# Two FFN output products computed as seven block products each, in a diffusion layer on one core

## The chip, the cores and the metric

The kernel runs on one core of a Trainium2 chip. Its engines are TensorE (PE; its weight loads are shown apart as PEld), VectorE (DVE), ScalarE (ACT), GpSimd (POOL) and SyncE (SP), which here issues all DMAs. The metric is the device time of one execution in microseconds (us); lower is better. For the kernel before, the median of three runs is 2811.78 us (2809.13 to 2812.79).

## The reference, cut to what matters

The program is one layer over 1024 latent tokens with a prefix of 256 context tokens, model width 1024, hidden width of the FFN 2816. All data is fp32. In short:

```python
def swiglu(h, w_in, w_out):
    a, b = jnp.split(h @ w_in, 2, axis=-1)
    return (jax.nn.silu(a) * b) @ w_out

x  = x  + 0.5 * ml[2] * swiglu(modulate(rms_norm(x,  norm1_g), ml[0], ml[1]), ffn1_w_in, ffn1_w_out)
cx = cx + 0.5 * mc[2] * swiglu(modulate(rms_norm(cx, norm1_g), mc[0], mc[1]), ffn1_w_in, ffn1_w_out)
...                     # short convolution and grouped-query attention, merged, added to x
x  = x  + 0.5 * ml[8] * swiglu(modulate(rms_norm(x,  norm3_g), ml[6], ml[7]), ffn2_w_in, ffn2_w_out)
return rms_norm(x, final_g)
```

`ml` and `mc` are nine rows of modulation, `silu(c) @ w_mod + b_mod`, for latent and context tokens. The change concerns the product with `w_out` (2816 x 1024) in the two FFNs over the latent tokens.

## The kernel before, in words

**Layout.** Activations lie transposed: 128 channels on the partitions, tokens along the free dimension. The 1024 tokens are two chunks of 512, C0 and C1. `x` has 8 blocks of 128 channels (KD = 8), the hidden activation `hid` has 22 (NH = 22).

**Precision.** Every fp32 operand is split into a high part (an ACT cast to the fp32r type) and a low part (a DVE subtraction) by `split` (line 186). A block product is three matmuls: high x high, high x low, low x high (`mm3`, line 218). One matmul multiplies a 128x128 block of weights with a 128x512 block of tokens into one PSUM bank.

**Buffers.** 38 tiles of 128x1024 with the tag `A` (`atile`) hold what lives long. `raw` has three buffers of that size for weights as loaded, `wh` and `wl` four each for split operands (W_BUFS, line 39), `t` eleven of 128x512. Of the eight PSUM banks, `ps_s` rotates over five, `ps_t` over two, `ps_o` has one (lines 121 to 128). A framework (Tile) places the semaphores and orders each engine's instructions, by the order of the program and by when an instruction can start in its own model; the queue of SP, which issues the DMAs, is in order as well.

**First halves of the FFNs.** `h @ w_in` is already a product of 2x2 blocks in seven block products (`class Winograd`, line 463): over the pair of column blocks of `w_in` that give `a` and `b`, the halves of the model width, and the two token chunks. `keep` holds the split sums of activations (r1 to r7, four `A` tiles each), `lefts` loads and prepares weights, with sums on GpSimd, `start` computes products 1 and 2 of the first few blocks while `norm1` still makes the other operands, and `second` and `third` do products 6, 7, 4, 5, 3 and add them up on DVE. Each product takes 12 matmuls.

**Second half of FFN 1** (lines 1026 to 1066). The hidden activation was spilled to DRAM (`spill`, line 963, into `hd`). For each token chunk, `hs` loads the 22 blocks of `hid` and splits them, once per chunk. Then, for three, three and two of the eight output blocks `ds`, one `ps_s` bank per block sums up 22 x 3 matmuls, with the weights loaded by `load_w` in columns of 128. An eviction on DVE (`scalar_tensor_tensor`: bank times gate plus `x`) writes `x`, which is stored to `xd`. Beside this the loop drives other work: `run(steps, 4)` in C0 finishes the modulation rows (`later_mod`, line 261: eight loads of 128x512, eight multiply-adds on DVE, two matmuls, per half row), and in C1 `run(norms2, 1)` makes the first operands of the mixing stage from C0 (`norm0`, line 499). After each C1 block, `mix.square(d)` (line 514) adds to the sum of squares that `norm1` (line 525) needs.

**FFN 2** (`ffn`, line 742, called in line 1522). Here the two halves are interleaved: for each of 11 pairs of hidden blocks, the seven products of `w_in` are done for two blocks, `hidden` splits the result and keeps it in SBUF, `out_pieces` (line 451) loads and splits the two row blocks of `w_out`, and for both chunks and all eight output blocks six matmuls go into a bank, which DVE adds to `x` times the gate at once. So `x` is evicted to once per pair, 176 times and more. For the last pair, C1 goes in two parts of 256 tokens (`last_chunks`), and `after2` starts the final norm of the parts that are done (`final`, line 1488): squares and scaled copies on ACT, additions on DVE and GpSimd, column sums on TensorE, a Newton iteration of small DVE operations, transposes on TensorE, scaling, and the store of the output.

The profile gives line 88 for nearly all instructions, because one helper issues them. Groups are told apart by tiles.

Of the kernel before, what the change touches and what calls it, by code (L numbers as in the profile page):

```python
# [9 lines left out]
F32 = mybir.dt.float32  # L10
# [3 lines left out]
ALU = mybir.AluOpType  # L14
# [35 lines left out]
def tile_dit_layer(  # L50
# [79 lines left out]
    def matmul(out, w, x, start, stop, pinned=False):  # L130
        inst = pe.matmul(out, w, x, start=start, stop=stop)
        if pinned:
            tc.keep_in_program_order(inst)
# [329 lines left out]
    class Winograd:  # L463
# [6 lines left out]
        def __init__(self, xs, gain, mod, m, pairs, plain=False, ahead=3, side_from=None):  # L470
# [9 lines left out]
            self.n_ahead, self.side, self.started, self.n_left = ahead, None, [], 0  # L480
            self.source, self.ready = self.lefts(pairs, side_from), []
# [32 lines left out]
        def square(self, d):  # L514

            if d == 0:
                self.acc = [ttile("sq_acc")]
            sq = self.acc[0] if d == 0 else ttile("sq")
            act.activation(out=sq, in_=self.xs(d, C1), func=AF.Square)
            if d == KD - 1:  # L520
                self.acc.append(sq)
            elif d:
                dve.tensor_add(out=self.acc[0], in0=self.acc[0], in1=sq)

# [217 lines left out]
        def ffn(self, w_o, gate, last_chunks, after):  # L742
            def hidden(a, b, j, ch):

                if j % 2 == 0:
                    t = atile("hid", (P, 2, 512), F32R)
                    g = t[:, 0], t[:, 1]
                else:
                    g = ttile("gh", dt=F32R), ttile("gl", dt=F32R)
                act.activation(out=a, in_=a, func=AF.Silu)  # L750
                dve.tensor_mul(out=a, in0=a, in1=b)
                split(a, *g)
                hid[j, ch] = g

            for pr in range(NH // 2):
                hid = {}
                js = (2 * pr, 2 * pr + 1)
                if pr == 0:
                    self.start(self.norm1())
                for j in js:  # L760
                    u, c = self.next_first()
                    v, b = self.second(u)
                    hidden(c, b, j, C0)
                    hidden(*self.third(u, v), j, C1)
                ws = out_pieces(w_o, js)
                if pr < NH // 2 - 1:
                    self.prefetch(3)
                for ch in (C0, C1) if pr < NH // 2 - 1 else last_chunks:
                    s, o, n = ch
                    full = (C0, C1)[o // 512]  # L770
                    a = o - full[1]
                    for dt in range(KD):
                        po = ps_s(n)
                        c = (dt % 4) * P
                        terms = []
                        for j in (2 * pr, 2 * pr + 1):
                            wt = ws[j, dt // 4]
                            gh, gl = hid[j, full]
                            terms.append((wt[:, 0, c : c + P], wt[:, 1, c : c + P], gh[:, a : a + n], gl[:, a : a + n]))
                        mm3(po, terms)  # L780
                        dve.scalar_tensor_tensor(
                            out=xs(dt, ch), in0=po, scalar=gate[:, dt : dt + 1], in1=xs(dt, ch),
                            op0=ALU.mult, op1=ALU.add,
                        )
                        if pr == NH // 2 - 1:
                            after(ch, dt)
# [242 lines left out]
    for ch in (C0, C1):  # L1029
        o = ch[1]  # L1030
        hs = []
        for j in range(NH):
# [542 lines left out]
```

## Time and profile before

| | before |
|---|---|
| median of 3 runs | 2811.78 us (2809.13 to 2812.79) |
| the profiled execution's own time | 2810.07 us |
| its span, from the first to the last instruction | 2808.1 us |
| mean granted TensorE clock | 0.984 |
| DMA | 302.96 MB, mean 108 GB/s |

How to read it: the page shows one execution. A row of a group gives the engine, the operation, output and inputs by the program's names, the shape, the count, then the busy time, the mean length of one, and the idle time of that engine just before, with what ended it. In a row of a window, each engine's busy time stands with its count of instructions, then the granted TensorE clock (1.00 is full), the share of time in which the DMA engines were busy, and GB/s. Matmuls overlap in the pipeline, so their price is taken from the number that run in a stretch in which TensorE is busy throughout. A row for a DMA ends with the median time from issue to landing. The lines themselves stand in the prediction.

### The profile page before, as it was taken

What the parts mean: (1) busy time and instruction counts of PE and PEld (TensorE: products, weight loads), DVE (VectorE), ACT (ScalarE), POOL (GpSimd) and SP (SyncE); (2) the same over time, 40 slices, a digit from 0 to 9 for tenths busy, and PEclk for the clock granted to TensorE, in tenths of its full rate; (3) what the DMA queues carried; (4) which work ended last, traced back from release to release, by engine and by line L of the source; (5) the groups of instructions that cost most, each with busy time, mean ns of one, the idle gap of its engine ahead of it and who ended that gap; (6) DMA issues with size and microseconds to landing.
All of it is one profiled execution on the core that took longest, in us unless ns stands there. A gap on an engine that the chain in (4) does not pass through costs nothing.

```text
span 2808.1 us, 37023 instructions
## 1 busy us (share of the span) xinstructions
PE 2719.5 (97%) x13741; PEld 2283.1 (81%) x13741; DVE 1953.1 (70%) x3194; ACT 1105.0 (39%) x2177; POOL 586.7 (21%) x458
## 2 busy tenths in 40 slices
PE   7898999999999989999999999999998999999998
PEld 4687988888888868888999888877886788888887
DVE  5887688877864397676568676675458766666667
ACT  4524333333433243323344665674235212332225
POOL 2541122121001063323123111000014221212111
PEclk8899999999999989999999999999999999999999
DMA  8364434445974333322312321002432311111111
GB/s 304 101 200 149 144 109 126 130 143 160 311 240 127 102 119 108 102 74 91 108 44 76 102 79 42 31 31 75 162 91 90 110 41 53 60 56 58 46 53 68
DMA packets 355229, 302.96 MB, mean 108 GB/s; under 512 B 25558, under 2 KB 284776, under 8 KB 355048
## 3 DMA queue, kind: packets, MB, share of 16 engines
q1 hardware_dynamic: 355048, 300.59, 33.3%
q8 instruction: 108, 1.77, 0.3%
q14 instruction: 73, 0.60, 0.1%
HBM read 251.73 MB, written 48.76 MB: 107 GB/s over the span
## 4 chain that ended last, share of the span: by engine, by line
PE 81%; DVE 11%; DMA 4%; issue 2%; ACT 2%; POOL 1%; SPq 1%; DVEq 0%; ACTq 0%; POOLq 0%
PE ps L88 71%; PE po L88 6%; PE pt L88 4%; DVE wl L88 2%; DVE r L88 1%; DMA rawm<-in_w_mod_dram 1%; DVE nt L88 1%; DVE macc L88 1%; DMA raw<-in_ffn_w_out_dram 1%; DVE wo L88 1%; DVE uc L88 1%; DVE u L88 1%; DMA hid<-hd 1%; DVE h L88 1%; SPq L88 1%
## 5 line engine op out<-in xcount | busy, mean ns | idle before, releaser
L88 PE MATMUL ps<-r,wl 128*128 128x512 f32 x5280 | 1240.9, 394 | 36.6 <-ACT wl L88 13.2
L88 PEld LDWEIGHTS ps<-r,wl 128*128 128x128 f32 x5280 | 994.8, 190 | 255.7 <-ACT wl L88 17.2
L88 ACT CAST wl<-s 128x512 fp32r<-128x512 f32 x256 | 158.6, 620 | 335.4 <-PE ps L88 273.3
L88 ACT CAST wl<-raw 128x512 fp32r<-128x512 f32 x230 | 142.4, 620 | 243.5 <-PE ps L88 162.4
L88 DVE TENSOR_TENSOR wl<-raw,wl 128x512 fp32r<-128x512 f32 x228 | 168.2, 738 | 98.3 <-ACT wl L88 97.2
L88 POOL TENSOR_TENSOR s<-raw,s 128x512 f32<-128x512 f32 x64 | 98.6, 1541 | 621.4 <-DVE wl L88 617.3
L88 DVE TENSOR_TENSOR wl<-s,wl 128x512 fp32r<-128x512 f32 x256 | 214.7, 840 | 11.6 <-ACT wl L88 9.8
L88 PE MATMUL ps<-hid,wh 128*128 128x512 f32 x704 | 217.3, 390 | 0.6 <-ACT wh L88 0.6
L88 DVE SCALAR_TENSOR_TENSOR x<-ps,gate_l,x 128x512 f32<-128x512 f32 (+1 forms) x200 | 141.0, 726 | 81.2 <-PE ps L88 81.0
L88 POOL TENSOR_TENSOR s<-raw 128x512 f32<-128x512 f32 x64 | 90.8, 1419 | 401.8 <-DMA raw<-in_ffn_w_in_dram 163.9
L88 ACT CAST wh<-raw 128x1024 fp32r<-128x1024 f32 (+2 forms) x92 | 89.4, 976 | 196.5 <-PE ps L88 162.6
L88 PEld LDWEIGHTS ps<-hid,wh 128*128 128x128 f32 x704 | 131.8, 188 | 29.2 <-ACT wh L88 1.3
L88 DVE SCALAR_TENSOR_TENSOR macc<-rawm,silu_c,macc 128x512 f32<-128x512 f32 x168 | 141.6, 861 | 11.9 <-DMA rawm<-in_w_mod_dram 10.5
L88 PE MATMUL ps<-hid,wo 128*128 128x512 f32 (+1 forms) x552 | 147.8, 381 | 1.8 <-DVE x L88 1.8
L88 DVE TENSOR_TENSOR u<-u,ps 128x512 f32<-128x512 f32 x168 | 114.5, 681 | 49.7 <-PE ps L88 48.1
L88 POOL TENSOR_TENSOR sq_acc<-sq_acc,sq 128x512 f32<-128x512 f32 (+1 forms) x33 | 41.5, 1258 | 505.3 <-ACT sq L88 504.4
L88 DVE TENSOR_TENSOR wl<-raw,wh 128x1024 fp32r<-128x1024 f32 (+1 forms) x84 | 99.9, 1190 | 64.1 <-ACT wh L88 62.8
L88 PE MATMUL ps<-wh,r 128*128 128x256 f32 x768 | 141.6, 285 | 0.0
L88 DVE TENSOR_TENSOR pts<-pt,pts 128x512 fp32r<-128x512 f32 x160 | 108.7, 687 | 42.6 <-ACT pts L88 41.4
L88 PE MATMUL ps<-hid,wl 128*128 128x512 f32 x352 | 136.5, 389 | 0.0
L88 PE MATMUL ps<-gh,wo 128*128 128x512 f32 (+1 forms) x368 | 135.0, 380 | 0.0
L88 DVE TENSOR_REDUCE m<-ps 128x1 f32<-128x512 f32 (+1 forms) x192 | 111.1, 596 | 27.1 <-PE ps L88 26.1
(260 smaller groups left out, 4922.6 us busy)
## 6 DMA issues: line engine op xcount, KB each, us to landing
raw<-in_ffn_w_in_dram SPq DMA_DIRECT2D x114, 512.0 KB, 3.9
raw<-in_ffn_w_out_dram SPq DMA_DIRECT2D x76, 512.0 KB, 4.6
rawm<-in_w_mod_dram SPq DMA_DIRECT2D x128, 256.0 KB, 4.2
raw<-in_w_in_dram SPq DMA_DIRECT2D x57, 512.0 KB, 4.2
hid<-hd SPq DMA_DIRECT2D x44, 256.0 KB, 6.1
rawm<-in_w_mod_dram SPq DMA_DIRECT2D x16, 512.0 KB, 7.9
xd<-x SPq DMA_DIRECT2D x32, 256.0 KB, 8.6
x<-xd SPq DMA_DIRECT2D x32, 256.0 KB, 5.7
```

The source lines that it names most:

```text
L88: inst = getattr(self.engine, name)(*args, **kw)
```

## The change

Both products `w_out^T x hid` become products of 2x2 blocks: rows of `w_out` (hidden blocks 0 to 10 and 11 to 21), columns of `w_out` (output blocks 0 to 3 and 4 to 7), and token chunks. Seven block products with sums of operands take the place of eight. A new function, `row_products`, does them in the order 1, 2, 5, 6, 7, 3, 4. Products 1, 6, 7 and 4 add up one on another in four `ps_s` banks (`chain`), read after each; products 2, 5 and 3 use the other four banks. `Rows` holds the hidden activation in SBUF, unsplit, in tiles of two row blocks. For each group of two row blocks (five, and one of a single block) `operands` loads parts of `w_out` (`part_of_w`), splits both operands into `wl` and `wh`, and makes the sums for later products on DVE, in place.

In FFN 1 the modulation steps that ran in the old loop move into the loop of the mixing stage, and `norm0` of that stage moves into product 4. In FFN 2 the hidden activation is now spilled to DRAM for all blocks first and loaded again; the seven products follow. The last product there is done in two halves of 256 tokens, with split operands kept in `A` tiles, and the final norm runs beside it. In `final`, the scaled copies go from ACT to DVE, the sums of squares from GpSimd to DVE and to more matmuls, and one of two banks changes.

```diff
+    def row_products(w, rows, add, after=lambda i, k: None, halves=False):
+        R, groups = P * rows.n, rows.groups
+        sums = {}
+        def part_of_w(k, m, lower, left):
+            t = wpool.tile([P, 2, 512], F32, tag="raw", name=uniq("raw"), bufs=3)[:, :m]
+            o, c = k * P + R * lower, 512 * (not left)
+            load(t, w[o : o + m * P, c : c + 512].rearrange("(a p) n -> p a n", p=P))
+            return t
...
+        def operands(i, k, m, tags=("wl", "wh")):
+            b11, b12, b21, b22 = (rows.t[k, v, c] for v in range(2) for c in (1, 0))
+            if i == 1:
+                left = part_of_w(k, m, 0, True)
+            elif i == 2:
+                left = part_of_w(k, m, 1, True)
+            elif i == 7:
+                left, a21 = part_of_w(k, m, 0, True), part_of_w(k, m, 0, False)
+                dve.tensor_sub(out=left, in0=left, in1=a21)
+            elif i == 4:
+                left = part_of_w(k, m, 1, False)
+            else:
+                left = sums[k]
+            right = {1: b11, 2: b21, 5: b11, 6: b11, 7: b12, 4: b11, 3: b22}[i]
+            l, r = parts(left, m, tags[0]), parts(right, m, tags[1])
+            if i == 1:
+                dve.tensor_sub(out=b11, in0=b12, in1=b11)
+            elif i == 2:
+                sums[k] = atile("ws", (P, 2, 512))[:, :m]
+                a21, a22 = part_of_w(k, m, 0, False), part_of_w(k, m, 1, False)
+                dve.tensor_add(out=sums[k], in0=a21, in1=a22)
+            elif i == 5:
+                a11 = part_of_w(k, m, 0, True)
+                dve.tensor_sub(out=sums[k], in0=sums[k], in1=a11)
+                dve.tensor_sub(out=b11, in0=b22, in1=b11)
+            elif i == 6:
+                a12 = part_of_w(k, m, 1, True)
+                dve.tensor_sub(out=sums[k], in0=a12, in1=sums[k])
+                dve.tensor_sub(out=b12, in0=b22, in1=b12)
+            elif i == 3:
+                dve.tensor_sub(out=b11, in0=b21, in1=b11)
+            return l, r
+        def steps_of(i, ps, k, m, l, r, a=0, n=512):
+            for e in range(m):
+                for d in range(4):
+                    wh, wl = (t[:, e, d * P : (d + 1) * P] for t in l)
+                    xh, xl = (t[:, e, a : a + n] for t in r)
+                    on = i in (6, 7, 4)
+                    matmul(ps[d], wh, xh, start=not on and k + e == 0, stop=False, on=on)
+                    matmul(ps[d], wh, xl, start=False, stop=False, on=on)
+                    matmul(ps[d], wl, xh, start=False, stop=k + e == rows.n - 1, on=on)
+        chain = [ps_s() for _ in range(4)]
+        for i in (1, 2, 5, 6, 7, 3):
+            ps = chain if i in (1, 6, 7) else [ps_s(), ps_t(), ps_t(), ps_o()]
+            for k, m in groups:
+                steps_of(i, ps, k, m, *operands(i, k, m))
+                after(i, k)
+            for d in range(4):
+                if i in (1, 2):
+                    add(d, C1, ps[d])
+                elif i == 5:
+                    add(d, C0, ps[d])
+                    add(d + 4, C0, ps[d])
+                elif i in (6, 3):
+                    add(d, C0, ps[d])
+                elif i == 7:
+                    add(d + 4, C0, ps[d])
+            after(i, rows.n)
...                      # then product 4, for FFN 2 in two halves of 256 tokens
@@ FFN 1
+    hs = Rows(NH // 2, "hid")
+    hs.fetch(hd)
...
+        if i == 4 and k in (0, 2, 4, 6):
+            run(norms2, 1)
+    row_products(ffn1_w_out[0], hs, add1, after1)
@@ the loop of the mixing stage
         run(normc2, 2)
+        run(steps, 9)
@@ FFN 2
-    fast.ffn(ffn2_w_out[0], gate3["l"], last_chunks, after2)
+    fast.start(fast.norm1())
+    for j in range(NH):
+        u, c = fast.next_first()
+        v, b = fast.second(u)
+        spill(c, b, j, C0)
+        spill(*fast.third(u, v), j, C1)
+    hs = Rows(NH // 2, "hid")
+    hs.fetch(hd)
...
+    def after3(i, k):
+        if i == 9 and k < NH // 2:
+            run(finals[0], 3)
+        if (i, k) == (8, NH // 2):
+            run(finals[0], 2)
+        if i == 9 and k >= 4 and k < NH // 2:
+            run(finals[1], 4)
+        if (i, k) == (9, NH // 2 - 1):
+            run(finals[2], 4)
+    row_products(ffn2_w_out[0], hs, add3, after3, halves=True)
```

More of the change, by code (lines that the diff above doesn't have):

```diff
@@ L740, in third @@
             return u, v
[L742 to L786, printed above, removed]
```

153 lines of the change are left out of this document (99 added, 54 removed).

## The prediction

> **What bounds the kernel now.** I read the page first: busy time by engine, the strip of granted clock, the chain that ended last.
>
> ```profile
> span 2808.1 us, 37023 instructions
> PE 2719.5 (97%) x13741; PEld 2283.1 (81%) x13741; DVE 1953.1 (70%) x3194; ACT 1105.0 (39%) x2177; POOL 586.7 (21%) x458
> PEclk8899999999999989999999999999999999999999
> GB/s 304 101 200 149 144 109 126 130 143 160 311 240 127 102 119 108 102 74 91 108 44 76 102 79 42 31 31 75 162 91 90 110 41 53 60 56 58 46 53 68
> PE 81%; DVE 11%; DMA 4%; issue 2%; ACT 2%; POOL 1%; SPq 1%; DVEq 0%; ACTq 0%; POOLq 0%
> ```
>
> TensorE is busy 97% of the span and carries 81% of the chain, nearly always at full clock. That is an average, so next come the windows, cut at the stages that the change touches: the first FFN's output product (722.8 to 966.8), the start and the body of the mixing stage, the start, body and end of the second FFN, and a stretch of 256-wide matmuls.
>
> ```profile
> core 0: us, PE busy (x) PEld busy (x) DVE busy (x) ACT busy (x) POOL busy (x), PEclk, DMA share, GB/s
> 722.80:966.80 244.00, 243.44 (x1079) 200.15 (x1078) 131.43 (x175) 83.22 (x112) 12.64 (x7) 1.00 0.62 198
> 966.80:1040.00 73.20, 60.95 (x242) 46.32 (x241) 59.81 (x83) 32.81 (x61) 36.31 (x26) 0.88 0.33 108
> 1040.00:1370.00 330.00, 330.00 (x1459) 273.15 (x1458) 238.68 (x357) 108.46 (x180) 107.64 (x75) 1.00 0.31 98
> 2107.20:2200.00 92.80, 79.48 (x331) 62.25 (x330) 78.27 (x104) 43.67 (x75) 37.48 (x25) 0.93 0.32 104
> 2200.00:2770.00 570.00, 569.54 (x2511) 470.70 (x2510) 375.93 (x539) 153.90 (x262) 103.08 (x75) 1.00 0.18 54
> 2770.00:2808.10 38.10, 30.05 (x215) 27.25 (x213) 29.00 (x78) 27.51 (x57) 8.54 (x9) 0.96 0.27 111
> 1450.00:1500.00 50.00, 50.00 (x422) 50.00 (x421) 40.49 (x109) 22.97 (x88) 17.74 (x37) 1.00 0.14 44
> ```
>
> Both output products run where TensorE never rests (243.44 of 244.00; 569.54 of 570.00). A matmul left out there is time gained, as long as the engines that feed it keep up. DVE is busy 131 of the first 244 us, 376 of the 570. For the price of a 512-wide matmul I want a stretch that holds little else:
>
> ```profile
> 2600.00:2650.00 50.00, 50.00 (x222) 41.42 (x221) 31.30 (x46) 15.95 (x27) 7.15 (x6) 1.00 0.18 53
> ```
>
> 50.00 / 222 = **0.225 us** per 512-wide matmul, and 50.00 / 422 = **0.118 us** per 256-wide one (the row 1450 to 1500). The 389 ns that the groups below show for one is its length in the pipeline, not its price.
>
> **The change part by part.** First the matmuls that exist now, by shape:
>
> ```profile
> L88 PE MATMUL ps<-hid,wh x704: 387/389/504, 722.8 to 966.2; 128*128 128x512 f32 x176
> L88 PE MATMUL ps<-hid,wl x352: 387/389/398, 724.3 to 966.4; 128*128 128x512 f32 x176
> L88 PE MATMUL ps<-hid,wo 128*128 128x512 f32 x504 | 139.3, 390 | 1.8 <-DVE x L88 1.8
> L88 PE MATMUL ps<-gh,wo 128*128 128x512 f32 x336 | 126.7, 389 | 0.0
> L88 PE MATMUL ps<-gl,wo 128*128 128x512 f32 x168 | 64.9, 389 | 0.0
> L88 PE MATMUL ps<-hid,wo 128*128 128x256 f32 x48 | 8.5, 286 | 0.0
> ```
>
> FFN 1: 704 + 352 = 1056 of width 512. FFN 2: 504 + 336 + 168 = 1008 of width 512 and 96 of width 256 (48 in the row, 48 with the other two operands). After: each of seven products has 11 row blocks x 4 column blocks x 3 terms = 132 matmuls, 924 in all. In FFN 2 the last product runs in two 256-wide halves: 792 + 264.
>
> - FFN 1: (1056 - 924) x 0.225 = **-29.7 us**.
> - FFN 2: (1008 - 792) x 0.225 = 48.6, less (264 - 96) x 0.118 = 19.8: **-28.8 us**.
>
> That is -58.5 us if TensorE stays as busy as now. What feeds it decides the rest:
>
> ```profile
> L88 DVE TENSOR_TENSOR wl<-raw,wh 128x1024 fp32r<-128x1024 f32 x68 | 84.5, 1245 | 30.3 <-ACT wh L88 29.1
> L88 ACT CAST wh<-raw 128x1024 fp32r<-128x1024 f32 x68 | 71.2, 1051 | 148.2 <-PE ps L88 120.7 <-DMA raw<-in_ffn_w_out_dram 15.0 <-DMA raw<-in_w_in_dram 8.0
> L88 DVE SCALAR_TENSOR_TENSOR x<-ps,gate_l,x 128x512 f32<-128x512 f32 x184 | 133.5, 748 | 80.1 <-PE ps L88 80.1
> raw<-in_ffn_w_out_dram SPq DMA_DIRECT2D x76, 512.0 KB, 4.6
> rawm<-in_w_mod_dram SPq DMA_DIRECT2D x16, 512.0 KB, 7.9
> hid<-hd SPq DMA_DIRECT2D x44, 256.0 KB, 6.1
> ```
>
> A product is 5.5 groups of two row blocks; a group is 24 matmuls, 5.4 us. Only two groups fit the four `wl` and four `wh` buffers, so the feed may lag by one group at most.
>
> *DVE.* Each group takes two subtractions for the low parts, and sums that prepare later products: 3, 3, 4, 4, 3, 3 and 2 operations of 1024 elements in products 1, 2, 5, 6, 7, 3, 4. That is 22 x 5.5 x 1.245 = 151 us, and 32 evictions of 0.748 us make 24: 175 of 208 us. It fits as a whole. In 5 and 6 it doesn't: 4 x 5.5 x 1.245 = 27.4, plus 4 evictions of product 2 (30.4) and 8 of product 5 (33.4), against 29.7 of matmuls. The excess is 4.4 us; part of it is hidden by the lead. I take 2 (bounds 0 and 4.4). ACT casts 14 x 5.5 x 1.051 = 81 us: not a bound.
>
> *Loads.* Product 2 loads three pieces of `w` per group (its own operand and the two of the sum) through three `raw` buffers. Each buffer's round is landing 4.6 + cast 1.05 + subtraction 1.25 = 6.9 us, against 5.4: 1.5 x 5.5 = 8 us late, less up to one group of lead. I take 5 (bounds 0 and, with the 7.9 us row, 21). Product 7 loads two: one buffer is held for 4.6 + 1.25 + 1.05 + 1.25 = 8.2 us, the other for 4.6 + 1.25 = 5.9; over three buffers that is 14.1 / 3 = 4.7 us per group, just under 5.4. I take 1. On SP's queue these loads stand behind the `xd` stores in FFN 1, which wait for evictions; that wait is in the bounds.
>
> For the landing, the Trainium skill, "DMA: Bandwidth & Descriptors", Anatomy of one DMA — SWDGE (gpsimd) path, gives 2.0 us plus bytes over 436 GB/s, an estimate of 3.2 us here; by that product 2 would hide its loads and the sum would be 10 us lower for the two stages. It is fitted on another path, and the 4.6 us row is what I go by.
>
> *Handovers.* Product 5 takes over the banks of 2, and 7 goes on in those of 6. The last group has 12 matmuls in four banks, so bank 0 is done 9 x 0.225 = 2.0 us before the end, and evictions of 0.748 us follow the matmuls at nearly their pace. The new wait stands on TensorE with all later matmuls behind it; it costs little only if DVE is free at that moment. I take 3 per stage, the stage's entry with it (bounds 0 and 11: four evictions, then a load of 6.1 and its split). At the entry of FFN 2 the `hid` tiles need slots of the 38 `A` tiles: 8 hold `x`, 28 hold `r`, so the loads start as the last block's `r` come free, ahead of need in the order of product 1.
>
> *Clock.* 1 us per stage, since waits this short left the clock at 1.00 in the rows above.
>
> New waits: 2 + 5 + 1 + 3 + 1 = **12 us per stage, +24**.
>
> *Around the stages.* (a) FFN 1's stage is now 244.0 for 1056 x 0.225 = 237.6 us; of the other 6.4, 23 more matmuls take about half (six of full width and smaller ones, an estimate), and about 3 us are waits, which my 12 replace: **-3**. (b) The last 63 steps of the modulations move into the mixing body: three half rows, 24 operations on DVE by this row, and 24 loads of 256 KB on SP:
>
> ```profile
> L88 DVE SCALAR_TENSOR_TENSOR macc<-rawm,silu_c,macc 128x512 f32<-128x512 f32 x168 | 141.6, 861 | 11.9 <-DMA rawm<-in_w_mod_dram 10.5
> ```
>
> 24 x 0.861 = 21 us beside 330 us in which DVE is busy 239. TensorE hides it; if that cover is gone it costs 21. **+2**. (c) `norm0` of the mixing stage is squeezed from the second column chunk's 122 us (half of 244) into product 4's 30, and four squares come after the last matmul instead of one: its start, which already loses time (60.95 of 73.20, clock 0.88), begins later: **+3** (bounds 0 and 10). (d) In FFN 2 the first half now runs unbroken; the hidden splits and 184 evictions leave DVE, two loads and stores of `hd` are added and hide under matmuls: 0. (e) The end: four adds in place of one after the last matmul, but fewer additions of squares: 0 (bounds -2 and +4).
>
> Sum against the profiled execution: 2808.1 - 58.5 + 24 - 3 + 2 + 3 = 2775.6 us of span. That execution took 2810.07 us, 2.0 above its span, and the median shown is 1.7 above that: 2775.6 + 3.7 = **2779 us**.
>
> **The rivals.**
>
> *All hidden.* The loads run ahead and DVE's lag is covered; only entries, handovers and the clock cost, 4 per stage instead of 12, and (b) is free: 2775.6 - 16 - 2 + 3.7 = **2761**. For it: the mixing body runs at 330.00 of 330.00 with the same kind of feed. Against it: product 2 asks for 1.5 MB in 5.4 us, 290 GB/s, and the densest slices of the strip (around this stage, and at the kernel's start) moved 311 and 304.
>
> *The `raw` ring binds (slower).* If three loads in flight land in 7.9 us, product 2's round is 10.2 against 5.4 and costs 4.8 x 5.5 - 5.4 = 21; product 7's is (11.4 + 9.1) / 3 = 6.9 and costs 8. That is 23 more per stage than I took: **2825**. Against 2811.78 it decides from a landing of about 6.8 us on, between the two rows. For it: 7.9 stands in this trace for loads of this size in a burst. Against it: those are the loads at the kernel's start, where many more than three are queued at once.
>
> *The clock falls.* Here waits on the feed coincide with a lower granted clock:
>
> ```profile
> 200.00:250.00 50.00, 40.30 (x182) 32.81 (x181) 42.03 (x79) 19.45 (x39) 17.59 (x16) 0.86 0.41 127
> 450.00:500.00 50.00, 49.37 (x280) 42.67 (x279) 38.12 (x61) 17.11 (x31) 8.38 (x5) 1.00 0.32 95
> 1000.00:1050.00 50.00, 41.43 (x145) 30.21 (x146) 45.29 (x65) 20.66 (x39) 29.10 (x22) 0.83 0.36 117
> ```
>
> At 80% busy the clock was 0.86 and 0.83, at 99% it was 1.00. If products 2 and 7 run at 0.85, their 59 us of matmuls take 10.5 more per stage: 2779 + 21 = **2800**. The Trainium skill, "TensorE: Matmul & The Clock Gate", A second HAM failure mode: psum-queue depth-cycling, says that cycling through PSUM banks with short rests between groups made the clock swing; it speaks for this case. Against it: the present stage also changes banks, and stood at 1.00.
>
> *It doesn't do what it says*: fewer matmuls are certain from the code; I give it nothing.
>
> **How the numbers follow.** Forecast (2765 to 2795) 0.51, all hidden 0.21, clock falls 0.12, ring binds 0.16. About 0.2% (6 us) is what a measurement of this kernel can tell from no change. Ring bound ends within 0.2% in a fifth of its cases: 0.03; the clock case is nearly always faster. So faster 0.82, same 0.04, slower 0.14. The range takes in the hidden case and most of the ring's: 2754 to 2822.
>
> **What would show it.** Matmuls: 924 per stage, TensorE's idle time there mostly before product 2, with `raw` loads ending it, then before 5 and 7 with evictions ending it. DVE near 85% busy in the stage and close to full in products 5 and 6. The stage's length near 222 us instead of 244. A landing of `raw` above 6.8 us, or a granted clock below 0.95 in the stages, would make the prediction wrong upward; a stage below 213 us, downward.

## The result, and the profile after

| | before | after |
|---|---|---|
| median of 20 runs each | 2813.21 us (2809.13 to 2821.24) | 2817.73 us (2814.79 to 2824.51) |
| span of the profiled execution | 2808.1 us | 2814.9 us |
| mean granted TensorE clock | 0.984 | 0.979 |

The ratio of after to before is 1.002, 95% interval 1.0014 to 1.0026. The kernel became about 0.2% slower. The time lies in the range on record, but the forecast had said faster. Against the forecast span of 2775.6 us, 39.3 us have to be found.

The page of the kernel after: span, TensorE's busy time, its granted clock in 40 slices, and the chain that ended last.

```profile
span 2814.9 us, 36971 instructions
PE 2689.3 (96%) x13625; PEld 2253.9 (80%) x13625; DVE 2014.9 (72%) x3166; ACT 1129.9 (40%) x2141; POOL 582.5 (21%) x449
PEclk8899999999999989999999999999999999999999
PE 77%; DVE 11%; DMA 6%; issue 3%; ACT 2%; POOL 1%; SPq 1%; DVEq 0%; ACTq 0%; POOLq 0%
```

TensorE is busy 30 us less (2719.5 before), and yet the span is 7 us longer: its idle time grew by 37 us, from 88.6 to 125.6. Where, is read from four marks on TensorE: the first and last matmul of FFN 1's output product, the first matmul after the mixing loop (operand `h2ch`), and the last before FFN 2 (operand `mh`). Rows by tile, with the first and last start in us; the kernel after:

```profile
L88 PE MATMUL ps<-wh,wl x627: 387/389/629, 724.0 to 959.4; 128*128 128x512 f32 x157
L88 PE MATMUL pt<-wh,wl x198: 387/389/628, 757.6 to 926.3; 128*128 128x512 f32 x198
L88 PE MATMUL po<-wh,wl x99: 388/389/398, 758.5 to 926.7; 128*128 128x512 f32 x99
L88 PE MATMUL ps<-wh,h2ch x32: 278/283/363, 1387.0 to 1421.4; 128*128 128x256 f32 x32
L88 PE MATMUL ps<-mh,wl x128: 387/389/477, 2033.5 to 2121.3; 128*128 128x512 f32 x128
```

The same two marks in the kernel before:

```profile
L88 PE MATMUL ps<-wh,h2ch x32: 277/283/363, 1372.2 to 1406.4; 128*128 128x256 f32 x32
L88 PE MATMUL ps<-mh,wl x128: 387/389/477, 2019.2 to 2106.9; 128*128 128x512 f32 x128
```

627 + 198 + 99 = 924 matmuls: the count is as forecast. The stretches between the marks (before: 722.8, 966.4, 1372.2, 2106.9, 2808.1):

| stretch | before | forecast | after | missed by |
|---|---|---|---|---|
| up to the output product | 722.8 | 722.8 | 724.0 | +1.2 |
| FFN 1's output product | 243.6 | 222.9 (−29.7 + 12 − 3) | 235.4 | **+12.5** |
| start and loop of the mixing stage | 405.8 | 410.8 (+2 + 3) | 427.6 | **+16.8** |
| from there to FFN 2 | 734.7 | 734.7 | 734.3 | −0.4 |
| FFN 2 and the end | 701.2 | 684.4 (−28.8 + 12) | 693.6 | **+9.2** |

The largest single miss is not in a product that the change rewrites, but in the mixing stage behind the first. The two products together miss 21.7 us. TensorE's busy and idle time in the three stretches that changed (the windows between the same marks, in us):

| stretch | busy before | busy after | idle before | idle after |
|---|---|---|---|---|
| FFN 1's output product | 243.04 | 218.34 | 0.56 | 17.06 |
| start and loop of the mixing stage | 393.55 | 401.24 | 12.25 | 26.36 |
| FFN 2 and the end | 679.37 | 665.39 | 21.83 | 28.21 |

In the mixing stage the same 1680 matmuls of full width run before and after, so there TensorE lost 14.1 us to longer rests and 7.7 us to more busy time: dearer matmuls, and eight small ones that came with the moved steps. Windows of the kernel after (columns as in the prediction): FFN 1's products 1, 2, 5, 6, 7, 3, 4, each from its first matmul to the first of the next, then the mixing stage, then FFN 2's product 2.

```profile
724.00:757.10 33.10, 30.75 (x134) 24.54 (x133) 31.12 (x36) 11.71 (x13) 0.00 (x0) 1.00 0.97 364
757.10:798.10 41.00, 31.71 (x133) 24.21 (x132) 26.32 (x33) 12.32 (x14) 0.00 (x0) 1.00 0.65 229
798.10:829.80 31.70, 31.63 (x132) 26.04 (x133) 28.28 (x30) 11.66 (x15) 0.00 (x0) 0.95 0.46 153
829.80:864.30 34.50, 31.99 (x133) 25.66 (x131) 32.03 (x35) 11.53 (x13) 0.00 (x0) 0.95 0.30 100
864.30:895.60 31.30, 30.52 (x132) 24.87 (x133) 20.72 (x21) 11.07 (x12) 0.00 (x0) 1.00 0.51 168
895.60:926.90 31.30, 30.25 (x133) 24.69 (x133) 15.68 (x17) 11.16 (x12) 0.00 (x0) 1.00 0.09 34
926.90:959.80 32.90, 31.86 (x146) 25.83 (x144) 28.33 (x43) 21.25 (x31) 6.46 (x3) 1.00 0.38 120
960.00:1000.00 40.00, 33.17 (x140) 26.60 (x140) 30.44 (x46) 19.56 (x36) 14.58 (x10) 0.91 0.37 119
1000.00:1040.00 40.00, 28.51 (x95) 19.34 (x96) 35.55 (x43) 17.64 (x34) 24.62 (x18) 0.83 0.30 99
1040.00:1060.00 20.00, 14.07 (x52) 11.01 (x51) 15.54 (x30) 5.09 (x8) 6.13 (x4) 0.83 0.35 109
1060.00:1370.00 310.00, 308.12 (x1356) 253.06 (x1355) 238.56 (x353) 101.56 (x172) 104.58 (x73) 1.00 0.35 111
2590.00:2625.10 35.10, 31.94 (x134) 25.64 (x132) 23.02 (x24) 12.29 (x13) 0.00 (x0) 0.95 0.65 221
```

A product without waits takes 132 x 0.225 = 29.7 us. Product 2 took 41.0 in FFN 1 and 35.1 in FFN 2; FFN 1's products 1 and 6 took 33.1 and 34.5. In the mixing stage most is lost before 1060. From 1060 to 1370 TensorE runs nearly as before: 1356 matmuls, where the kernel before does 1369 in the same window, 13 fewer or 2.9 us. In the kernel before, the stretch from 1040 on was full (330.00 of 330.00).

What ended TensorE's waits in FFN 1's output product (722 to 962) of the kernel after: total us, times, the longest.

```profile
PE ps L88 <- ACT wl L88: 8.1, 6, 2.8
PE ps L88 <- DVE wh L88: 5.0, 4, 2.3
PE ps L88 <- DVE x L88: 3.8, 2, 3.6
PE ps L88 <- DVE wl L88: 1.0, 2, 0.9
```

That is 17.9 us, most of it at casts (5.6 of the 8.1 in product 2) and at the changes of product. The rest of the stage's surplus is mainly dearer matmuls: TensorE's busy time in the seven windows is 218.70 us for 943 matmuls, 0.232 each, 6.5 us more than at 0.225.

The landings stayed short. DMA issues on the page after:

```profile
raw<-in_ffn_w_out_dram SPq DMA_DIRECT2D x112, 512.0 KB, 4.0
hid<-hd SPq DMA_DIRECT2D x40, 512.0 KB, 6.8
```

### The profile page after: what moved, and what is told of

Its sections match the earlier page's. It is cut to its first block, busy times and chain, and to the rows that moved or that the text cites. A ratio compares the mean times of both kernels' runs of the same rounds, so it can differ in the third digit from the quotient of the medians.

```text
span 2814.9 us, 36971 instructions
## 1 busy us (share of the span) xinstructions
PE 2689.3 (96%) x13625; PEld 2253.9 (80%) x13625; DVE 2014.9 (72%) x3166; ACT 1129.9 (40%) x2141; POOL 582.5 (21%) x449
## 4 chain that ended last, share of the span: by engine, by line
PE 77%; DVE 11%; DMA 6%; issue 3%; ACT 2%; POOL 1%; SPq 1%; DVEq 0%; ACTq 0%; POOLq 0%
PE ps L88 64%; PE po L88 7%; PE pt L88 6%; DMA raw<-in_ffn_w_out_dram 3%; DVE wl L88 2%; DVE macc L88 1%; DVE nt L88 1%; DVE r L88 1%; DMA rawm<-in_w_mod_dram 1%; DVE x L88 1%; POOL s L88 1%; DVE h L88 1%; SPq L88 1%; DVE wh L88 0%; DVE ws L88 0%
## 5 line engine op out<-in xcount | busy, mean ns | idle before, releaser
L88 ACT CAST wl<-raw 128x512 fp32r<-128x512 f32 (+1 forms) x272 | 183.4, 676 | 370.3 <-PE ps L88 230.6
L88 PE MATMUL ps<-wh,wl 128*128 128x512 f32 x1122 | 281.3, 397 | 27.4 <-DVE wh L88 10.7
L88 DVE TENSOR_TENSOR wl<-raw,wl 128x512 fp32r<-128x512 f32 (+1 forms) x270 | 216.9, 805 | 110.1 <-ACT wl L88 104.2
L88 PEld LDWEIGHTS ps<-wh,wl 128*128 128x128 f32 x1122 | 211.6, 190 | 79.7 <-DVE wh L88 14.2
L88 DVE TENSOR_TENSOR u<-u,ps 128x512 f32<-128x512 f32 x168 | 114.3, 680 | 40.9 <-PE ps L88 40.5
L88 ACT CAST pts<-pt 128x512 fp32r<-128x512 f32 x160 | 93.0, 592 | 86.8 <-PE pt L88 85.0
L88 PEld LDWEIGHTS ps<-wh,r 128*128 128x128 f32 x768 | 120.7, 192 | 0.0
L88 PE MATMUL po<-pts,vh 128*128 128x512 f32 x256 | 110.3, 437 | 1.5 <-ACT pts L88 1.5
L88 PE MATMUL pt<-wh,wl 128*128 128x512 f32 x396 | 109.2, 397 | 0.1
L88 PE MATMUL ps<-wl,r 128*128 128x256 f32 x384 | 108.9, 284 | 0.0
L88 PE MATMUL ps<-kl,qs 128*128 128x512 f32 x384 | 106.0, 397 | 0.4 <-ACT pc L88 0.4
```

Of the source, the lines that this page charges most:

```text
L88: inst = getattr(self.engine, name)(*args, **kw)
```

## The experiments

Three stretches of each profiled execution, with the marks above; "before" is the kernel before on the same chip in the same session. The four sessions of the experiments have medians of 2812.85, 2813.28, 2813.49 and 2813.05 us for it. A stretch comes from one execution, and executions of one kernel differ (e8's five: 2798.84 to 2805.70), so a difference of 2 or 3 us between two stretches can be chance.

| kernel | median us | ratio to before, interval | FFN 1's product | mixing | FFN 2 |
|---|---|---|---|---|---|
| before | 2813.21 | | 243.6 | 405.8 | 701.2 |
| after | 2817.73 | 1.002 (1.0014 to 1.0026) | 235.4 | 427.6 | 693.6 |
| e1 steps alone | 2821.48 | 1.0026 (1.0016 to 1.0036) | 240.7 | 419.0 | 701.3 |
| e2 steps early | 2847.05 | 1.0121 (1.0105 to 1.0136) | 235.6 | 413.6 | 692.7 |
| e3 FFN 1 alone | 2823.13 | 1.0036 (1.0023 to 1.0049) | 236.2 | 427.9 | 701.1 |
| e4 FFN 2 alone | 2807.00 | 0.9981 (0.9971 to 0.999) | 243.7 | 406.0 | 693.2 |
| e5 steps later | 2808.98 | 0.9985 (0.9975 to 0.9994) | 235.8 | 418.5 | 695.2 |
| e6 sum in place | 2810.01 | 0.9991 (0.9982 to 1.0) | 229.4 | 427.4 | 693.2 |
| e7 context later | 2815.85 | 1.0012 (1.0003 to 1.0021) | 236.6 | 423.2 | 693.3 |
| e8 three edits | 2803.48 | 0.9964 (0.9951 to 0.9976) | 232.9 | 416.0 | 692.1 |
| e9 sums on GpSimd | 2815.11 | 1.0004 (0.9995 to 1.0013) | 241.0 | 416.8 | 694.8 |
| e10 seven started | 2792.17 | 0.9923 (0.991 to 0.9937) | 232.2 | 408.9 | 691.5 |
| e11 ten started | 2794.10 | 0.9928 (0.9916 to 0.994) | 231.2 | 406.3 | 692.6 |
| e12 sums left out | 2790.31 | 0.9918 (0.9905 to 0.9931) | 229.8 | 410.6 | 695.2 |

**The theory** from these rows: the moved modulation steps stall the mixing loop, not by DVE's time but by the order of the queues; the `raw` ring delays product 2; `norm1` starts the mixing stage late. The main rival for the first: the mixing stage is slow only because its norms come late, and the steps are covered.

### e1: the steps alone

The kernel before, with nothing changed but the place of the steps.

```diff
-                        run(steps, 4)
-                        run(steps)
@@ the loop of the mixing stage
+        run(steps, 9)
...                      # and run(steps) behind that loop, for what is left
```

> The kernel before with one part of the change alone: the last modulation steps leave the loop of FFN 1's output product and run in the loop of the mixing stage. Theory A (the moved steps stall the queues of ACT, DVE and GpSimd there: they wait for a matmul behind 46 others): about 10 us slower than before, with TensorE idle some 10 us between the first norm and 1100 us. Rival B (TensorE hides the steps, as the prediction had it, and the mixing stage loses time only because it starts with late operands): within 2 us of before.

The mixing stage went from 405.8 to 419.0: **+13.2**, of which 7.3 are TensorE's rests (12.25 to 19.52) and 5.9 its busy time (393.55 to 399.48). The output product, freed of the steps, gained 2.9. The rival fell. How it happens is in the order of time. First the kernel after (start, length, engine, operation, and in brackets the idle time before it and what ended it):

```profile
1030.62 12.69 PE L88 MATMUL ps<-r,wl 128*128 128x512 f32 x46 [0.50 <-ACT wl L88]
...
1043.52 0.40 PE L88 MATMUL pt<-acch,ones_r 128*1 128x512 f32 x1
...
1044.23 0.58 ACT L88 COPY mrow<-pt 1x512 f32<-1x512 f32 x1 [7.48 <-PE pt L88]
```

The end of a half row of the modulations is two tiny matmuls (`acch`, `accl`) and a copy on ACT. They stand on TensorE behind 46 matmuls of the mixing loop. ACT, in order, sits 7.48 us at the copy, and every cast of `wl` is behind it. Behind the copy ACT waits 5.49 us more, for an operation of DVE (`b`), so the copy is the first part of the delay and not all of it. Eight us after the copy TensorE has run out of weights:

```profile
1052.79 1.65 PE L88 MATMUL ps<-r,wl 128*128 128x512 f32 x3 [5.93 <-ACT wl L88]
```

The same two lines in e1, in which neither FFN product is changed:

```profile
1039.17 0.58 ACT L88 COPY mrow<-pt 1x512 f32<-1x512 f32 x1 [5.21 <-PE pt L88]
...
1048.06 4.22 PE L88 MATMUL ps<-r,wl 128*128 128x512 f32 x11 [3.54 <-ACT wl L88]
```

Over four runs the two waits go together: the copy waits 7.48, 5.21, 4.74 and 0.15 us in the kernel after, e1, e7 and e5, and TensorE then waits 5.93, 3.54, 3.36 and, in e5, not at all in the 13 us that follow. The rest of the 13.2 us, the matmuls that got dearer above all, is not traced to single instructions.

### e2: the steps before the stage

The kernel after, with the steps done in the first FFN's first half and none in the mixing loop.

```diff
-STEPS = (0, 6, 6, 6, 7, 7, 8, 8, 8, 15)
+STEPS = (0, 6, 6, 6, 7, 7, 8, 8, 8, 20)
@@ ahead of FFN 1's output product
+    run(steps)
@@ the loop of the mixing stage
-        run(steps, 9)
```

> The changed kernel with all modulation steps done in the first stage (20 per block instead of 15) and none in the mixing loop. Theory A: 8 to 12 us faster than the changed kernel, less 2 to 4 that the fuller first stage may cost, so about 2807; the mixing stage takes near 414 us instead of 426. Rival B: within 2 us of the changed kernel, 2816.

The mixing stage fell to 413.6, as expected, but the whole became 2847.05, where about 2807 was expected: the first half took 42 us more, since the steps delay it even more than the loop. Two findings hold. Without any step the mixing stage is still 7.8 us over the kernel before, and 6.3 us of these are lost by about its 50th matmul of full width (19.5 us after the stage's first mark, 13.2 in the kernel before), so it is the late start. And the steps are 427.6 − 413.6 = 14.0, which agrees with the 13.2 of e1. With e1's figure, 21.0 of the 21.8 us that the stage lost are found by two separate runs.

### e3 and e4: one FFN at a time

e3 has FFN 1 of the kernel after, steps and mixing stage with it, and FFN 2 of the kernel before; e4 the other way round.

```diff
-    row_products(ffn2_w_out[0], hs, add3, after3, halves=True)
+    fast.ffn(ffn2_w_out[0], gate3["l"], last_chunks, after2)
```

> The change in FFN 1 alone, with FFN 2 as before. Theory A (the loss of FFN 1's part: its stage gains 7 us, and the mixing stage gives 21 back): 13 to 15 us slower than before. Rival C (FFN 2's spill to DRAM and its tail are what eats the gain): not slower than before.

> The change in FFN 2 alone, with FFN 1 and the modulation steps as before. Theory A: 7 to 9 us faster than before (693.6 against 701.2 us from the last matmul of the stage ahead to the end). Rival C: as slow as the changed kernel, 3 to 6 us over before.

FFN 1 alone costs 10.3 us, FFN 2 alone gains 5.9. Both signs are theory A's, and both sizes fall short of it (13 to 15, and 7 to 9). The sum of both, +4.4, is what the change does (+4.5). The stretches are those of the kernel after, part by part, so the two do not act on each other by more than these runs can tell.

### e5, e6, e7: one repair each, on the kernel after

e5 leaves the steps out of the loop's first turn:

```diff
-        run(steps, 9)
+        if i:
+            run(steps, 9)
```

> The changed kernel with the moved modulation steps left out of the first turn of the mixing loop (7 x 9 steps instead of 8 x 9). Theory A (the stall is one place: in the first turn a copy on ACT waits 7.5 us for two small matmuls that stand behind 46 others, and the casts of the next weights stand behind the copy): 7 to 10 us faster than the changed kernel, about 2808. Rival B (the steps cost wherever they run beside the mixing stage, by DVE's time): within 2 us of the changed kernel.

The mixing stage went from 427.6 to 418.5, and the time to 2808.98. The first turn, in which the norms also compete, carries most of the steps' cost: 9.1 of 14.0 us. The same 24 multiply-adds run on DVE in this stage, 24.5 us of its time against 23.2, so DVE's total isn't the price.

e6 loads one piece of product 2's sum straight into the tile of the sum, so the ring of three has two loads per group, not three:

```diff
-                a21, a22 = part_of_w(k, m, 0, False), part_of_w(k, m, 1, False)
-                dve.tensor_add(out=sums[k], in0=a21, in1=a22)
+                load(sums[k], w[k * P : (k + m) * P, 512:].rearrange("(a p) n -> p a n", p=P))
+                a22 = part_of_w(k, m, 1, False)
+                dve.tensor_add(out=sums[k], in0=sums[k], in1=a22)
```

> The changed kernel with one of product 2's three loads taken out of the ring of raw buffers: it lands in the tile of the sum. Theory D (the ring of three buffers paces product 2, 6.5 us per group against 5.4): product 2 shorter by 5 to 8 us in FFN 1 (42.4 now) and by 2 to 4 in FFN 2 (34.2 now), about 2808 in all. Rival E (product 2 waits for the rate of the DMAs, which are busy with hid, x and weights at the entry): product 2 within 2 us of now, no change in the time.

The output product went from 235.4 to 229.4. In e6, FFN 1's product 2:

```profile
756.60:793.00 36.40, 32.17 (x134) 25.55 (x133) 24.96 (x32) 10.70 (x12) 0.00 (x0) 0.95 0.73 257
```

36.4 us instead of 41.0, with the same bytes (the 42.4 of the expectation is by other marks): the ring's size cost 4.6 us here, at a landing of 4 us. In FFN 2 product 2 went from 35.1 to 31.7, yet FFN 2 as a whole gained only 0.4: from product 3's first matmul to product 4's last it took 76.3 us in place of 73.0, for which no run gives a reason.

e7 moves the update of the context residual, whose stores stand on SP's queue between the `raw` loads of product 2, further back:

```diff
+        if (i, k) == (7, 0):
+            context_residual()
```

> The changed kernel with the update of the context residual (four loads, eight operations on DVE, four stores) moved from ahead of the products into product 7. Theory E (its stores wait for DVE on SP's queue, and its transfers fall into the densest stretch, so product 2's loads come late): product 2 of FFN 1 shorter by 3 to 5 us. Rival D (the ring alone paces product 2): within 1 us of now.

Product 2 did not get shorter (40.9 us, 759.2 to 800.1), so these stores don't pace it. The edit did less than it says: the framework placed the update in product 5 (809 to 815), not in 7, and product 5 became 32.8 us long where it was 31.7. The 1.9 us gained can't be assigned.

### e8: the three together

> The changed kernel with the three edits together: steps from the second turn on, one load of product 2 outside the ring, the context residual in product 7. If the three causes are separate, their gains add up: 15 to 20 us faster than the changed kernel, about 2799, and 12 to 15 faster than the kernel before. If D and E are one cause, about 2804.

2803.48 us, 14.2 below the kernel after; the three gains alone were 8.7, 7.7 and 1.9, 18.3 in sum. The 15 to 20 us of separate causes did not come, and the time stands at the 2804 of D and E as one cause. But the interval of this ratio alone is 3.5 us to either side, so it isn't shown whether the gains add up. One part of the shortfall is seen: the update of the context residual now runs in product 5, and that took 34.0 us (31.6 in e6).

### e9 and e12: does DVE's full queue pace products 5 and 6?

e9 is e8 with two sums per group on GpSimd; e12 is e10 with them left out, so that its products 6 and 7 multiply other numbers.

```diff
-                dve.tensor_sub(out=b11, in0=b22, in1=b11)
+                pool.tensor_sub(out=b11, in0=b22, in1=b11)
...
-                dve.tensor_sub(out=b12, in0=b22, in1=b12)
+                pool.tensor_sub(out=b12, in0=b22, in1=b12)
```

> On top of the kernel with three edits (2803.48 us, ratio 0.9964): the two sums of token operands that products 5 and 6 prepare (b22 - b11, b22 - b12) go from DVE to GpSimd, which is idle in those products. That takes 11 operations of 1.13 us mean, 12.4 us, off DVE per stage; on GpSimd, where 512 elements take 1.5 us, each takes about 3 us, 33 us over two products of 66, and they are needed only one product later. Theory A (DVE's full queue paces products 5 and 6, 31.88 of 33.00 and 32.34 of 34.00 us busy): the stretch from the first matmul of product 5 to the end of product 6 falls by 2 to 4 us per stage, 2796 to 2800 us in all (ratio 0.994 to 0.995). Theory B (DVE and GpSimd slow each other, as elsewhere in this kernel where DVE's 512-wide sums take 1.77 us instead of 0.68 beside GpSimd; or the waits there are handovers alone): no gain, 2803 us or above.

e9 took 11.6 us more than e8. In the order of time, e9 in product 5:

```profile
798.82 2.40 POOL L88 TENSOR_TENSOR hid<-hid,hid 128x1024 f32<-128x1024 f32 x1 [38.81 <-DVE wh L88]
799.32 2.99 DVE L88 TENSOR_TENSOR ws<-ws,raw 128x1024 f32<-128x1024 f32 x1
...
805.32 2.78 POOL L88 TENSOR_TENSOR hid<-hid,hid 128x1024 f32<-128x1024 f32 x1 [4.09 <-DVE wh L88]
805.77 3.42 DVE L88 TENSOR_TENSOR ws<-ws,raw 128x1024 f32<-128x1024 f32 x1
```

GpSimd ends at 801.22 and at 808.10; DVE's operation ends 1.09 us after each, about the 1.22 us that it takes alone. So DVE did nothing until GpSimd was done. The Trainium skill, "SBUF — State Buffer", section SBUF: two separate sides, says that the two engines share a pair of ports under an exclusive lock, which a DVE operation with two SBUF inputs needs against a GpSimd operation that reads SBUF; these rows agree. The framework also moved the six sums that belong to product 6 ahead into product 1, where they meet DVE's splits: in FFN 1 product 1 became 38.5 us long (33.1 in e8) and product 5 37.9 (34.0). So e9 could not answer the question, and e12 asks it without GpSimd.

> On top of the kernel with three edits and seven started blocks (2792.17 us, ratio 0.9923): this kernel leaves out the two sums of token operands that products 5 and 6 prepare (b22 - b11, b22 - b12), so products 6 and 7 multiply other numbers; the same matmuls, casts and loads run. DVE loses 11 operations of 1.13 us, 12.4 us, per stage. Theory A (DVE's full queue paces products 5 and 6): from the first matmul of product 5 to the first of product 7 takes 60 to 63 us instead of 67.6 in FFN 1 and 60 to 62 instead of 65.0 in FFN 2, 2780 to 2786 us in all (ratio 0.988 to 0.990). Theory B (only the handovers of banks cost there, evictions at DVE's own place in the queue): at most 1 us less per product, 2789 to 2792 us (ratio 0.991 to 0.9925).

With 12.4 us of DVE's work gone per stage, 2790.31 us stands against 2792.17, and the intervals overlap. e12's profiled execution is the longest of its five (2795.73), so its products are compared, not its span: from the first matmul of product 5 to the first of 7 it took 67.0 us in FFN 1 (67.6 in e10) and 65.9 in FFN 2 (65.0). **Theory A fell**: DVE's fullness is not what paces products 5 and 6. What is left at the start of product 5 in e12:

```profile
788.45 1.05 ACT L88 CAST wl<-ws 128x1024 fp32r<-128x1024 f32 x1 [4.94 <-PE po L88]
...
789.53 1.23 DVE L88 TENSOR_TENSOR wl<-ws,wl 128x1024 fp32r<-128x1024 f32 x1 [4.58 <-ACT wl L88]
790.67 0.74 DVE L88 SCALAR_TENSOR_TENSOR x<-ps,gate_l,x 128x512 f32<-128x512 f32 x1
```

DVE is idle 4.58 us before the split of product 5, because ACT's cast waited 4.94 us for a `wl` buffer that matmuls of product 2 still held; then splits and evictions come one after another. The last group of a product has one row block, 12 matmuls, 2.7 us, and covers little of that chain. This is read from the rows; it was not tried with more buffers or another group size, so it stays argued.

### e10 and e11: more lead at the start of the mixing stage

```diff
-RESIDENT, AH2, AH3 = 2, 5, 6
+RESIDENT, AH2, AH3 = 2, 7, 6
```

> On top of the kernel with three edits (2803.48 us, ratio 0.9964): the mixing stage starts products 1 and 2 of seven blocks ahead of norm1's operands instead of five (AH2 from 5 to 7). That is no more or less work, except that two more pairs of started sums go to DRAM and back. Theory A (the start of the mixing stage, still 9 us longer than in the kernel before, waits for norm1, whose squares now come four at a time after the last matmul of the output product, and two more blocks give TensorE 10.8 us of work to cover it): the mixing stage falls from 414.6 us to 407 to 411, 2796 to 2800 us in all (ratio 0.994 to 0.9955). Theory B (the feed itself is late there: casts and subtractions on ACT and DVE stand behind the norm's operations in their queues, so more started blocks wait as well): no gain, within 2 us of 2803, or slower by what is put aside.

e10 (on e8) takes **2792.17 us, ratio 0.9923 (0.991 to 0.9937)**, the fastest here that computes the whole layer, and 0.9% below the kernel after. The mixing stage fell from 416.0 to 408.9. The reason is not quite the expected one. e8, the whole stage and the part with the rests:

```profile
954.70:1370.70 416.00, 397.96 (x1717) 323.21 (x1717) 335.92 (x485) 151.74 (x260) 153.73 (x104) 0.97 0.37 117
985.00:1040.00 55.00, 40.66 (x137) 29.56 (x137) 49.52 (x63) 24.39 (x44) 35.57 (x25) 0.78 0.27 91
```

and e10:

```profile
954.30:1363.20 408.90, 390.42 (x1716) 320.25 (x1715) 328.63 (x485) 150.68 (x260) 157.38 (x104) 0.98 0.40 126
1000.00:1020.00 20.00, 5.08 (x11) 3.59 (x12) 18.80 (x18) 9.99 (x18) 14.90 (x10) 0.58 0.25 86
1020.00:1060.00 40.00, 40.00 (x179) 32.95 (x179) 35.14 (x60) 14.14 (x27) 20.37 (x16) 0.99 0.42 131
```

TensorE rests 18.0 us in e8 and 18.5 in e10, so it rests as long. But for the same 1680 matmuls of full width it is busy 7.5 us less in e10, which is the whole gain. In e8 the rests are spread over 55 us at a mean clock of 0.78; in e10 most of them are one piece of 15.2 us, 20 us at 0.58, and the clock is back at once (0.99 from 1020 on).

> On top of the kernel with three edits and seven started blocks (2792.17 us, ratio 0.9923): ten started blocks (AH2 from 7 to 10). With seven, TensorE's idle time at the start of the mixing stage is one piece of 15.2 us in place of several (18.5 us in all, as 18.0 before), and the granted clock is below 1.00 only from 1000 to 1020. Theory A (the lead covers the wait for norm1): three more blocks are 16 us more of cover, the piece of 15.2 us shrinks to under 5, 2780 to 2786 us (ratio 0.988 to 0.990). Theory B (the idle time only moves to the end of the lead, since the casts that it waits for stand behind the norm's and the started blocks' operations in ACT's and DVE's queues; the gain of the step to seven was the clock alone): one piece of about 15 us again, 2790 to 2797 us (ratio 0.9915 to 0.994), three more blocks put aside in DRAM.

Ten started blocks gave 2794.10, no different from seven. The time is where theory B put it, but the sign is theory A's: the piece of 15.2 us is gone, and from 950 to 1060 TensorE waits 6.3 us in all. The whole stage in e11:

```profile
954.80:1361.10 406.30, 394.93 (x1716) 321.02 (x1715) 336.09 (x485) 148.85 (x260) 155.99 (x104) 0.99 0.43 138
```

It rests 11.4 us, 7.1 less than in e10, but its matmuls take 4.5 us more, and 5.1 us of the rests now lie between 1060 and 1200, where e10 has none. So the lead did cover the wait for `norm1`, and dearer matmuls and new rests behind it took most of that back; why these came stays open. The profiled executions differ by 1.7 us in span (2787.7 and 2789.4), the other way round than the medians, so the two kernels can't be told apart.

## Why the prediction was wrong, point by point

**The matmuls held, their price did not.** The counts are as forecast (924 in FFN 1; 792 and 264 half as wide in FFN 2), but TensorE's busy time fell by 30.2 us and not by 58.5: by 24.7 in FFN 1's product for 29.7, by 14.0 in FFN 2 for 28.8, and in the mixing stage it rose by 7.7.

**The step that failed: (b), "TensorE hides it. +2", with 21 as its bound.** I priced the moved steps by DVE's time, 24 x 0.861 us, and looked for cover on TensorE. DVE's total was not the price: in e5 it is no smaller, and the stage is 9.1 us shorter. Each half row ends in two matmuls and a copy that the in-order queues tie together: ACT waits 7.48 us for two matmuls behind 46 others, and the casts that feed TensorE stand behind it. It cost 13.2 us alone (e1) and 14.0 in the changed kernel (e2), 12.0 more than my 2. It is the largest part of the 39.3 us and not the whole: by an estimate, 2817.73 − 12.0, the kernel would have come to about 2806 without it, faster, and still far from 2779. My own rule, to name what is queued behind a waiting instruction, I applied to the added waits and not to the moved ones.

**The ring, 5 per stage, was mis-sized in FFN 1.** The mechanism held: two loads per group instead of three gave 6.0 us of the stage back (e6). TensorE's waits in FFN 1's product 2, in the order of time:

```profile
764.13 0.50 PE L88 MATMUL ps<-wh,wl 128*128 128x512 f32 x1 [1.35 <-ACT wl L88]
...
773.19 0.74 PE L88 MATMUL ps<-wh,wl 128*128 128x512 f32 x2 [2.83 <-ACT wl L88]
...
779.59 0.73 PE L88 MATMUL ps<-wh,wl 128*128 128x512 f32 x2 [0.62 <-ACT wl L88]
...
786.16 0.73 PE L88 MATMUL ps<-wh,wl 128*128 128x512 f32 x2 [0.84 <-ACT wl L88]
```

These are the starts of groups 2 to 5. Once it runs, a group takes 6.4 and 6.6 us; I had estimated a round of 6.9. But the first two groups took 7.0 (from 757.1) and 9.1, 5.3 us over two times 5.4. I had taken off one group of lead, 5.4 us, and there was next to none. SP's queue in the kernel after:

```profile
746.39 1.62 SPq L88 DMA_DIRECT2D raw<-in_ffn_w_out_dram  x3
...
756.07 1.52 SPq L88 DMA_DIRECT2D raw<-in_ffn_w_out_dram  x2
```

One of the first three loads is product 1's last. With them the ring is full, and the next load is issued 1.1 us before product 2 begins: SP waited 4.5 us for the subtraction of product 1's last group, which frees a buffer. That subtraction was late: its load stood behind those of `x` and was cast only at 752.43, in the densest stretch (product 1 moves 364 GB/s at a DMA share of 0.97, as `hid` and `x` are fetched there). This is read from the rows; no run separated the full ring from the dense stretch. In FFN 2 the groups after the first ran at 5.4 each: there the ring did not bind, and product 2 lost its 5 us at the start. The landing was not the error: with 4.0 us in my own sum a round is 4.0 + 1.05 + 1.25 = 6.3 us, 5 us over a product, near the 6.4 and 6.6 of the rows. By the estimate on record from the Trainium skill, "DMA: Bandwidth & Descriptors", Anatomy of one DMA — SWDGE (gpsimd) path (3.2 us), the loads would have hidden; the 4.0 of the page of the profile is above it, and they did not.

**Handovers and DVE's lag, 3 + 2.** The waits for DVE, 5.0 + 3.8 + 1.0, are 9.8 us in FFN 1. The longest is at the change from product 2 to 5, in the kernel after:

```profile
795.54 0.69 DVE L88 TENSOR_TENSOR ws<-raw,raw 128x512 f32<-128x512 f32 x1 [1.52 <-DMA raw<-in_ffn_w_out_dram]
796.15 1.22 DVE L88 TENSOR_TENSOR wh<-hid,wh 128x1024 fp32r<-128x1024 f32 x1
797.28 0.74 DVE L88 SCALAR_TENSOR_TENSOR x<-ps,gate_l,x 128x512 f32<-128x512 f32 x1
...
798.17 2.21 PE L88 MATMUL ps<-wh,wl 128*128 128x512 f32 x7 [3.56 <-DVE x L88]
```

The eviction that frees the bank stands behind a sum that waits for a late load: ring and handover are one chain here. DVE was busy 28.28 of 31.70 and 32.03 of 34.50 us in products 5 and 6, near to full as I had said (182.48 of 235.80, 77%, in the stage, where I had said 85%), but e12 showed that this fullness wasn't the price.

**The clock, 1 per stage.** FFN 1's matmuls cost 6.5 us more than their count (0.232 us each). The granted clock can be about 3 us of that, an estimate: 0.95 over the 63.6 busy us of products 5 and 6. Product 2 was as dear (31.71 us for 133) at a clock of 1.00, so the rest is something else, which stays open. The Trainium skill, "TensorE: Matmul & The Clock Gate", A second HAM failure mode: psum-queue depth-cycling, was on record for a falling clock; the trace shows little of it: 0.95 in two of seven windows.

**(a), −3**, came out in size by luck. There were no 3 us of waits to replace: TensorE was idle 0.56 us in the old stage, as my own row says (243.44 of 244.00). The old loop got 2.9 us shorter in e1 because that idle time and eight small matmuls of the steps left it; in the change these run in the mixing stage.

**(c), +3 within 0 to 10**, was 7.8 (e2), inside its bounds; more started blocks gave 7.1 back (e10), by cheaper matmuls and not by shorter rests.

**(d) and (e), 0 each.** FFN 2 lost 9.2 us more than forecast, and a term that I had put at nothing is most of it. The sums of squares of the final norm went to TensorE, 80 matmuls of 128x1 where there were 16:

```profile
2784.07 3.63 PE L88 MATMUL pt<-ones,sq 128*128 128x1 f32 x32
```

At this rate 64 more take about 7 us, an estimate. 56 of the 80 run between 2766.8 and 2798.7, where TensorE never rests, so there they lengthen the stage; the other 24 run in the tail. That is 16.1 us from the last output matmul (2798.7) to the end, where it was 12.9 (from 2795.2). No run took these matmuls out, so the estimate is not tested.

**The rivals.** Ring binds, given 0.16, is nearest in time (2825), and that is luck: its condition, a landing above 6.8 us, did not come (4.0). That the time lies in the range, which took in this rival, is luck as well. The clock in products 2 and 7, for the 2800 of the third rival, stood at 1.00 in FFN 1 and at 0.95 and 0.98 in FFN 2, not at 0.85. The case that came, that moved work stalls a stage which the change does not touch, was not among them.

## What to carry to other kernels

Work that is moved into a loop is priced by its waits, not by its engine time: follow each operation that crosses engines (a small matmul, then a copy) and ask what it stands behind on the one engine and what stands behind it on the other. A ring of buffers shared by loads of different use gives no lead while the stage before still holds its buffers, so load long-lived operands straight into their own tiles. Count the small matmuls that a change adds as well. And where rests couldn't be avoided, one long rest cost less here than many short ones (e8, e10).

## What the runs showed of the hardware

- DVE and GpSimd excluded each other for whole operations with both inputs in SBUF: 2.99 and 3.42 us instead of 1.22 (e9). Moving 24 sums from DVE to an idle GpSimd made the kernel 11.6 us slower.
- With nearly the same idle time (18.0 and 18.5 us), the same matmuls took 7.5 us less when most of it was one piece: mean clock 0.78 over 55 us against 0.58 over 20 us (e8, e10).
- At a DMA share of 0.97, one core moved 364 GB/s over 33.1 us with transfers of 512 KB and 256 KB.
